# A first expert picked by ranking, and a sort that runs among its weight pieces

## The chip, the core and the metric

The program runs on one core of a Trainium2 chip: TensorE (PE), VectorE (DVE), ScalarE (ACT), GpSimd (POOL), and SyncE (SP), which here only issues DMAs. The metric is the device time of one execution in microseconds (us); less is better. The kernel before has a median of 1737.5 us over three runs, 1734.37 to 1741.73.

## What is computed

One layer over 1024 tokens of 1024 features in float32: an input projection; three mixers side by side (retention, a state-space scan, windowed attention); an output projection with a residual and a norm; then sixteen experts, each of which chooses its own 128 tokens:

```
mix  = concat(retention, S5, windowed attention) @ W_out
h    = LN(alpha*h + mix)
aff  = softmax(h @ router_w)                  # 1024 tokens x 16 experts
gates, idx = top_k(aff of one expert, 128)    # for each expert
xs   = h[idx]
out  = (silu(xs @ w_gate) * (xs @ w_up)) @ w_down * gates
h    = LN(alpha*h + scatter_add(out, idx))
```

Which tokens an expert takes is known only when all 1024 affinities of that expert are. A tie goes to the lower token number.

## The kernel before

The tokens lie in eight tiles of 128. After the mixers a loop over half steps i runs attention_scores (i), attention_out (i - 1), out_proj_half (i - 4) and router (i - 9): the stages of one tile follow one another with these lags, and a scheduler at build time merges them into a fixed order on each engine. A matmul in float32 at full rate takes three passes over numbers split in a high and a low part (mm3, L78): ACT rounds the high part, DVE subtracts to get the low one (split, L67; lines L71 and L72). This is done to activations and to every weight.

attention_out (L780) divides the four heads' probabilities S by their sum on DVE (L790), turns them on PE and multiplies them with the values. out_proj_norm stores the normed rows to h1_dram and, times alpha, to acc_dram. router (L852) turns the normed tile and multiplies it with the router's weights.

When the loop has ended, top_k (L910) finds for all experts at once the 128th largest affinity: on DVE eight rounds of MAX8 and MATCH_REPLACE, bitonic merges (L886, L887), then transposes and products on PE that give each token its slot. expert_hot and expert_slots turn slots into token numbers, expert_gather (L1005) fetches the 128 rows of one expert by an indirect DMA on POOL's queue, turned (L1019) transposes them on PE and tokens splits them into xT.

The experts' order is written by hand (Experts, L1043). Weights come as 384 pieces of 1 MB; of each quarter of an expert four pieces are for gate and up (tile gu), and two for the down projection (tile y) of the quarter before. load(k) issues the DMA of piece k on SP's queue into a raw buffer, and cut(k) splits it into a whl buffer, of which there are six. quarter (L1145) runs a piece's twelve matmuls on PE, then cuts the piece six further on. start (L1093) loads eight pieces and cuts six before the first; the low parts of the first three are done by POOL (POOL_FIRST = 3), the others by DVE. plan puts the other steps (silu, hid, its turn to hT, the next expert's tokens) between the pieces.

Of the kernel before, what the change touches and what calls it, by code (L numbers as in the profile page):

```python
# [779 lines left out]
def attention_out(K, i):  # L780
# [71 lines left out]
def router(K, t):  # L852
    nc, pool = K.nc, K.op
    z = K.Y.pop(t)[2]
    hT = K.rt.pop(t)[:, 1, :].rearrange("p (c f) -> p c f", c=KC)
    for q in range(2):
        pt = K.ptp.tile([P, 4, P], F32, name="tp")
        for c in range(4):
            nc.tensor.transpose(pt[:, c, :], z[:, (q * 4 + c) * P:(q * 4 + c + 1) * P], K.ident)
        if q == 0 or t < NT - 1:  # L860
            nc.scalar.activation(hT[:, q * 4:q * 4 + 4, :], pt, AF.Copy)
        else:
            nc.vector.tensor_copy(hT[:, q * 4:q * 4 + 4, :], pt)
    pr = K.psm.tile([P, P], F32, name="sm")
    for c in range(KC):
        nc.tensor.matmul(pr[0:E, :], K.rw[:, c, :], hT[:, c, :], start=(c == 0), stop=(c == KC - 1))  # L866
    lT = pool.tile([E, P], F32, name="lT", bufs=2)
    nc.vector.tensor_copy(lT, pr[0:E, :])
    pl = K.psm.tile([P, E], F32, name="sm")
    nc.tensor.transpose(pl, lT, K.ident[0:E, 0:E])  # L870
    s = pool.tile([P, 4], F32, name="rsm", bufs=2)
    a = pool.tile([P, E], F32, name="aff", bufs=2)
    nc.vector.tensor_reduce(s[:, 0:1], pl, AX.X, OP.max)
    nc.vector.tensor_scalar(s[:, 1:2], s[:, 0:1], -1.0, None, op0=OP.mult)
    nc.scalar.activation(a, pl, AF.Exp, bias=s[:, 1:2], accum_out=s[:, 2:3])
    nc.vector.reciprocal(s[:, 3:4], s[:, 2:3])
    nc.vector.tensor_scalar(K.aff[:, t, :], a, s[:, 3:4], None, op0=OP.mult)


def bitonic(K, pool, x, rows, k, name):  # L880

    nc = K.nc
# [27 lines left out]
def top_k(K):  # L910
# [5 lines left out]
    aff = K.aff.rearrange("p t e -> p (t e)")
    with K.tc.tile_pool(name="topk", bufs=1, side="left") as pool:
        pt = K.ptp.tile([P, 4, P], F32, name="tp")
        nc.tensor.transpose(pt[:, 0, :], aff, K.ident)
        rest = [K.aff] + [pool.tile([P, NT, E], F32, name=f"rest{i}") for i in range(2)]  # L920
        for i in range(3):
            nc.gpsimd.tensor_copy(K.tok[:, :, :, 2 + i], rest[i])
            if i < 2:
                nc.gpsimd.tensor_tensor(rest[i + 1], rest[i], K.tok[:, :, :, 2 + i], OP.subtract)
        w = [[pool.tile([P, 64], F32, name=f"w{h}{i}") for i in range(2)] for h in range(2)]
        half = [pool.tile([P, 64], F32, name=f"half{h}") for h in range(2)]
        for h in range(2):
            nc.vector.tensor_copy(w[h][0], pt[:, 0, h * 64:(h + 1) * 64])
        for i in range(8):
            for h in range(2):  # L930
                nc.vector.max(half[h][:, i * 8:i * 8 + 8], w[h][i % 2])
            for h in range(2):
                if i < 7:
                    nc.vector.match_replace(w[h][1 - i % 2], half[h][:, i * 8:i * 8 + 8], w[h][i % 2], -1.0)
        both = pool.tile([P, P], F32, name="both")
        nc.vector.tensor_tensor(both[:, 0:64], half[0], half[1][:, ::-1], OP.max)
        nc.vector.tensor_tensor(both[:, 64:P], half[0], half[1][:, ::-1], OP.min)
        top = bitonic(K, pool, both, P, 32, "b128")
        for rows in (64, 32):
            o = pool.tile([rows, P], F32, name=f"o{rows}")  # L940
            nc.vector.tensor_copy(o, top[rows:2 * rows, ::-1])
            m = pool.tile([rows, P], F32, name=f"m{rows}")
            nc.vector.tensor_tensor(m, top[0:rows], o, OP.max)
            top = bitonic(K, pool, m, rows, 64, f"b{rows}")
        rev = pool.tile([32, P], F32, name="rev")
        nc.vector.tensor_copy(rev, top[:, ::-1])
        pt = K.ptp.tile([P, 4, P], F32, name="tp")
        nc.tensor.transpose(pt[:, 0, 0:32], top, K.ident[0:32, 0:32])
        nc.tensor.transpose(pt[:, 1, 0:32], rev, K.ident[0:32, 0:32])
        m = pool.tile([P, 2, E], F32, name="mm")  # L950
        nc.vector.tensor_copy(m[:, 0, :], pt[:, 0, 0:E])
        nc.vector.tensor_tensor(m[:, 1, :], m[:, 0, :], pt[:, 1, E:2 * E], OP.max)
        pt = K.ptp.tile([P, 4, P], F32, name="tp")
        nc.tensor.transpose(pt[0:E, 0, :], m[:, 1, :], K.ident)
        tau = pool.tile([E, 1], F32, name="tau")
        nc.vector.tensor_reduce(tau, pt[0:E, 0, :], AX.X, OP.min)
        taus = pool.tile([E, P], F32, name="taus")
        nc.vector.tensor_copy(taus, tau.to_broadcast([E, P]))
        pt = K.ptp.tile([P, 4, P], F32, name="tp")
        nc.tensor.transpose(pt[:, 0, 0:E], taus, K.ident[0:E, 0:E])  # L960
        g = pool.tile([P, 2, NT, E], BF16, name="g")
        for i, op in ((0, OP.is_gt), (1, OP.is_equal)):
            nc.vector.tensor_tensor(g[:, i], K.aff, pt[:, 0, None, 0:E].to_broadcast([P, NT, E]), op)

        pp = K.pmm.tile([P, 512], F32, name="mm")
        before = pp[:, 0:2 * NT * E].rearrange("p (a t e) -> p a t e", a=2, e=E)
        n = pp[:, 2 * NT * E:2 * NT * E + E]
        nc.tensor.matmul(pp[:, 0:2 * NT * E], K.order01[:, 0, :], g.rearrange("p a t e -> p (a t e)"),
                         start=True, stop=False)
        for s in range(1, NT):  # L970
            nc.tensor.matmul(before[:, :, s:, :], K.order01[:, 1, :], g[:, :, 0:NT - s, :],
                             start=False, stop=(s == NT - 1))
        pn = K.psm.tile([P, E], F32, name="sm")
        for t in range(NT):
            nc.tensor.matmul(pn, K.order01[:, 1, :], g[:, 0, t, :], start=(t == 0), stop=(t == NT - 1))
        w = pool.tile([P, 4, NT, E], F32, name="sl")
        nc.vector.tensor_copy(w[:, 0], before[:, 0])
        nc.vector.tensor_copy(w[:, 3, 0], pn)
        nc.vector.tensor_tensor(w[:, 1], before[:, 1], w[:, 3, 0:1].to_broadcast([P, NT, E]), OP.add)
        nc.vector.tensor_tensor(w[:, 0], w[:, 0], w[:, 1], OP.subtract)  # L980
        nc.vector.tensor_tensor(w[:, 0], w[:, 0], g[:, 0], OP.mult)
        nc.vector.tensor_tensor(w[:, 1], w[:, 1], w[:, 0], OP.add)
# [544 lines left out]
```

## Time and profile before

| | |
|---|---|
| median of three runs | 1737.5 us |
| the profiled execution | 1739.56 us |
| its span, first to last instruction | 1737.9 us |
| attention and projection loop | about 360 to 527 us |
| last routers, sort, first gather | 527 to 585 us |
| experts | 585 to 1720 us |

Times in the rows are microseconds from the start of the span. PE's busy time counts pipelined matmuls whose ends are modelled, so it can be full while single matmuls are further apart than they need to be. A chain row gives what the end of the program can be followed back to.

### The profile page before, as it was taken

Reading aid. Unit: us, or ns where it says so; the run is one execution under the profiler, and the core shown is the slowest. Engines: PE = TensorE matmul, PEld = TensorE weight load, DVE = VectorE, ACT = ScalarE, POOL = GpSimd, SP = SyncE. Lnnn points to the kernel's source line nnn. Section 1 sums busy time; section 2 is a strip of 40 time slices with the busy share of each in tenths; the row PEclk is TensorE's granted clock in tenths of the full one; section 3 lists DMA queues with packets and bytes.
Section 4 is the critical chain, followed back from the end, with each engine's and each line's share of the span. In section 5 each row is a group of like instructions: output and inputs, shape, how many; then the busy total and the mean of one; then the engine's idle time right before and its main releaser. Section 6 shows DMA issues by size and latency. Waiting matters only on the chain.

```text
span 1737.9 us, 21027 instructions
## 1 busy us (share of the span) xinstructions
PE 1608.6 (93%) x7673; PEld 1294.0 (74%) x7673; DVE 1435.3 (83%) x1678; ACT 1058.7 (61%) x1082; POOL 335.5 (19%) x403
## 2 busy tenths in 40 slices
PE   6898996899993599999999999999999999999996
PEld 4688875577772488888888888888888778778785
DVE  8687962678867688888888889888898999989995
ACT  3332331455543377777777777777777777777772
POOL 6926801001003101011010010110101213121121
PEclk9999898999997699999999999999999999999998
DMA  6353189652225399999999999999999999999993
GB/s 246 115 143 102 51 244 267 196 176 74 77 105 242 113 337 370 371 387 356 382 377 370 383 362 376 382 371 383 366 372 409 384 396 412 382 406 376 394 402 138
DMA packets 110871, 512.53 MB, mean 295 GB/s; under 512 B 12336, under 2 KB 35120, under 8 KB 60080
## 3 DMA queue, kind: packets, MB, share of 16 engines
q1 hardware_dynamic: 100640, 481.31, 73.1%
q0 software_dynamic: 10128, 29.89, 5.6%
q8 instruction: 60, 0.98, 0.2%
q14 instruction: 43, 0.35, 0.1%
HBM read 465.01 MB, written 46.14 MB: 294 GB/s over the span
## 4 chain that ended last, share of the span: by engine, by line
PE 58%; DVE 14%; DMA 12%; issue 7%; ACT 4%; POOL 3%; SPq 1%; POOLq 0%; DVEq 0%; ACTq 0%
PE gu L1038 28%; PE y L1038 13%; DVE whl L72 5%; DMA zz<-acc_d 4%; PE mm L80 3%; PE mm L82 3%; PE mm L81 3%; ACT whl L71 2%; DMA wraw<-in_exp_w_down 2%; DMA wraw<-in_exp_w_up 2%; PE tp L1023 2%; PE tp L796 1%; PE sm L866 1%; PE po L81 1%; PE po L82 1%
## 5 line engine op out<-in xcount | busy, mean ns | idle before, releaser
L72 DVE TENSOR_TENSOR whl<-wraw,whl 128x2048 fp32r<-128x2048 f32 (+1 forms) x395 | 887.0, 2256 | 136.2 <-ACT whl L71 135.8
L71 ACT ACTIVATE whl<-wraw 128x2048 fp32r<-128x2048 f32 (+1 forms) x400 | 753.3, 1887 | 260.3 <-PE gu L1038 124.1
L1038 PE MATMUL gu<-whl,xT 128*128 128x512 f32 x3072 | 748.5, 400 | 0.0
L1038 PEld LDWEIGHTS gu<-whl,xT 128*128 128x128 f32 x3072 | 573.1, 189 | 130.7 <-ACT xT L71 0.3
L1038 PE MATMUL y<-whl,hT 128*128 128x512 f32 x1536 | 369.0, 396 | 0.7 <-ACT hT L71 0.7
L1038 PEld LDWEIGHTS y<-whl,hT 128*128 128x128 f32 x1536 | 288.6, 188 | 70.6 <-ACT hT L71 0.9
L1014 POOL DMA_INDIRECT xs<-h_d,index x16 | 44.8, 2798 | 755.9 <-issue 492.7
L80 PE MATMUL mm<-hT,whl 128*128 128x512 f32 x160 | 63.6, 398 | 6.2 <-DVE qst L75 5.3
L82 PE MATMUL mm<-hT,whl 128*128 128x512 f32 x160 | 63.1, 394 | 0.0
L81 PE MATMUL mm<-hT,whl 128*128 128x512 f32 x160 | 63.0, 393 | 0.0
L71 ACT ACTIVATE hT<-tp 128x512 fp32r<-128x512 f32 x80 | 46.4, 585 | 24.5 <-PE tp L141 15.4
L72 DVE TENSOR_TENSOR hT<-tp,hT 128x512 fp32r<-128x512 f32 x80 | 54.2, 681 | 7.1 <-ACT hT L71 7.1
L80 PE MATMUL mm<-WO,yh 128*128 128x512 f32 x128 | 51.2, 400 | 2.7 <-ACT yh L71 2.7
L80 PE MATMUL mm<-whl,hT 128*128 128x512 f32 (+1 forms) x128 | 47.3, 371 | 4.2 <-ACT gate L326 1.8
L81 PE MATMUL mm<-WO,yh 128*128 128x512 f32 x128 | 50.4, 393 | 0.0
L82 PE MATMUL mm<-WO,yl 128*128 128x512 f32 x128 | 50.1, 398 | 0.0
L1023 PE MATMUL tp<-ident,hid 128*128 128x128 f32 x256 | 38.8, 274 | 9.2 <-DVE hid L1122 9.1
L1023 PEld LDWEIGHTS tp<-ident,hid 128*128 128x128 f32 x256 | 31.2, 140 | 20.4 <-DVE hid L1122 12.6
L82 PE MATMUL mm<-whl,hT 128*128 128x512 f32 (+1 forms) x128 | 46.3, 363 | 0.0
L81 PE MATMUL mm<-whl,hT 128*128 128x512 f32 (+1 forms) x128 | 46.3, 364 | 0.0
L776 ACT ACTIVATE S<-S,asm 128x384 f32<-128x384 f32 (+1 forms) x64 | 36.9, 579 | 12.5 <-DVE asm L772 12.4
L1122 DVE TENSOR_TENSOR hid<-hid,gu 128x512 f32<-128x512 f32 x64 | 43.5, 679 | 0.0
(386 smaller groups left out, 1832.1 us busy)
## 6 DMA issues: line engine op xcount, KB each, us to landing
wraw<-in_exp_w_gate SPq DMA_DIRECT2D x128, 1024.0 KB, 7.4
wraw<-in_exp_w_up SPq DMA_DIRECT2D x128, 1024.0 KB, 7.2
wraw<-in_exp_w_down SPq DMA_DIRECT2D x128, 1024.0 KB, 8.0
wraw<-in_w_in SPq DMA_DIRECT2D x8, 1024.0 KB, 6.3
x<-in_x SPq DMA_DIRECT2D x8, 512.0 KB, 5.0
h_d<-x SPq DMA_DIRECT2D x8, 512.0 KB, 2.9
wraw<-in_w_out SPq DMA_DIRECT2D x4, 1024.0 KB, 5.7
q_d<-qst SPq DMA_DIRECT2D x64, 64.0 KB, 3.6
```

What stands on the lines that cost most here:

```text
L71: nc.scalar.activation(hi, src, AF.Copy)
L72: eng.tensor_tensor(lo, src, hi.bitcast(F32), OP.subtract)
L80: nc.tensor.matmul(ps, a[0], b[0], start=start, stop=False)
L81: nc.tensor.matmul(ps, a[0], b[1], start=False, stop=False)
L82: nc.tensor.matmul(ps, a[1], b[0], start=False, stop=stop)
L776: nc.scalar.activation(S[g][:, :W], S[g][:, :W], AF.Exp, bias=nm[:, g:g + 1], accum_out=rs[:, g:g + 1])
L796: nc.tensor.transpose(pt[:, g, :], S[g][:, (b - b0) * P:(b - b0 + 1) * P], K.ident)
L866: nc.tensor.matmul(pr[0:E, :], K.rw[:, c, :], hT[:, c, :], start=(c == 0), stop=(c == KC - 1))
L1014: nc.gpsimd.indirect_dma_start(out=xs, out_offset=None, in_=K.h1_dram, in_offset=bass.IndirectOffsetOnAxis(ap=K.index[:, e:e + 1], axis=0))
L1023: K.nc.tensor.transpose(pt[:, c, :], src[:, (c0 + c) * P:(c0 + c + 1) * P], K.ident)
L1038: nc.tensor.matmul(ps, a[s][c], u[:, t, i * w:(i + 1) * w], start=first and id(ps) not in began, stop=last and left[id(ps)] == 0)
L1122: at(self.after, q, 3, lambda: nc.vector.tensor_tensor(self.h[q], self.h[q], self.pg[q][1], OP.mult))
```

## The change

Five parts, and a rearrangement of the loop that goes with them:

1. The router no longer waits for the norm: its weights are multiplied by the norm's gain once, and mean and deviation are applied to the 16 logits (affinities). The lags become 1, 3 and 5. The division of S goes from DVE to ACT.
2. For the first expert alone, each tile's tokens are ranked by counting how many tokens have a larger affinity (rank_tile). When seven tiles are counted, their best 128, the candidates, are fetched by an indirect DMA while PE still projects the last tile (candidates_ranked, candidates_fetched).
3. When the last tile's affinities are there, first_slots counts them against the candidates, and first_turned picks the 128 rows of the first expert out of the two tiles by products with one-hot matrices, which turns them at once.
4. cut is divided into high (ACT) and low (DVE), which run ahead by lead(n) pieces; the first pieces are cut in the last tile's section (last_tile), which is written in a fixed order.
5. top_k, now a generator, gives one slice of the sort of all experts after each piece of the first expert. The second expert's gather moves to the third quarter.

```
     for g in range(4):
-        nc.vector.tensor_scalar(S[g][:, :W], S[g][:, :W], rd[:, g:g + 1], None, op0=OP.mult)
+        nc.scalar.activation(S[g][:, :W], S[g][:, :W], AF.Copy, scale=rd[:, g:g + 1])
...
+def rank_before(K, row, t, col, own):
+    G = K.tk.tile([P, LT * P], BF16, name="G")[:, 0:row.shape[1]]
+    nc.vector.tensor_scalar(G, row, K.aff[:, t, 0:1], None, op0=OP.is_ge, op1=OP.add, accum_out=K.cnt[:, t, col:col + 1])
...
+def candidates_fetched(K):
+    for t in range(LT):
+        nc.tensor.matmul(pt[:, 0, 0:5], K.hot0[:, t, :], K.tok[:, t, 0, :], start=(t == 0), stop=(t == LT - 1))
...
+    nc.gpsimd.indirect_dma_start(out=K.xc, out_offset=None, in_=K.h1_dram[0:LT * P, :],
+                                 in_offset=bass.IndirectOffsetOnAxis(ap=index, axis=0))
...
+def first_turned(K, half):
+    src = (K.Y[LT][2], K.xc)
+    for c in range(4):
+        cs = slice((half * 4 + c) * P, (half * 4 + c + 1) * P)
+        for i in range(2):
+            K.nc.tensor.matmul(pt[:, c, :], src[i][:, cs], K.hits[i], start=(i == 0), stop=(i == 1))
...
+    def low(self, k):
+        while self.lows <= min(k, len(self.order) - 1):
+            k1, self.lows = self.lows, self.lows + 1
+            u, raw = self.whl[k1], self.raw.pop(k1).rearrange("p a b -> p (a b)")
+            self.K.nc.vector.tensor_tensor(u[:, 1, :], raw, u[:, 0, :].bitcast(F32), OP.subtract)
+            if k1 != 2:
+                self.load(k1 + (2 if k1 < 2 else 5))
...
+    def lead(self, n):
+        return 3 + sum(n >= i for i in (16, 30, 44))
...
-            self.cut(self.taken + self.RING)
+            if self.sort and next(self.sort, self) is self:
+                self.sort = None
+                K.sorted()
+            lead = self.taken + self.lead(self.taken)
+            self.high(min(lead + 1, self.taken + self.RING))
+            self.low(lead)
...
+def last_tile(K, I, O, pool, close):
...
+    affinities(K, t)
+    token_parts(K, t)
+    out_proj_part(K, LT, 0, 7, KC)
+    G = rank_tile(K, t)
+    out_proj_part(K, LT, 1, 0, 4)
+    router_turn(K, LT, 0)
+    candidates_ranked(K, G)
+    out_proj_part(K, LT, 1, 4, 6)
+    candidates_fetched(K)
+    router_part(K, LT, 0)
+    X.high(1)
+    out_proj_part(K, LT, 1, 6, KC)
+    out_proj_stats(K, LT)
...
+    first_slots(K)
+    out_proj_store(K, LT)
+    halves = [first_turned(K, half) for half in range(2)]
+    pt = first_numbers(K)
+    rows = top_k_rows(K)
+    X.low(1)
...
+    for half in range(2):
+        X.tokens(0, half, halves[half])
+        if half == 0:
+            for k in range(4, 8):
+                X.load(k)
+            X.high(3)
+    X.low(2)
+    expert_gather(K, 0, pt)
+    X.sort = top_k(K, rows)
```

In DVE's order before, from the end of the sort to the first expert's matmuls (sl and slot are the sort's last tiles, hot the one-hot tiles, slotc and index the token numbers):

```order
L984 SCALAR_TENSOR_TENSOR slot<-sl 128x128
L992 TENSOR_TENSOR hot<-slot,slots 128x512 x2
L1009 COPY slotc<-tp 128x5
L1010 TENSOR_TENSOR index<-slotc 128x1
L1011 TENSOR_TENSOR slotc<-slotc 128x1
L1012 TENSOR_TENSOR gates<-slotc 128x1
L72 TENSOR_TENSOR whl<-wraw,whl 128x2048 x3
L72 TENSOR_TENSOR xT_5480<-tp,xT_5479 128x512 x2
```

In DVE's order of the changed kernel, from the last hit tile into the sort (w and half are the sort's first tiles):

```order
L1100 TENSOR_SCALAR hit_5438<-slots,last 128x128
L1303 TENSOR_TENSOR whl<-wraw,whl 128x2048
L71 TENSOR_TENSOR xT_5495<-tp,xT_5494 128x512 x2
L1303 TENSOR_TENSOR whl<-wraw,whl 128x2048
...
L1148 MATCH_REPLACE w_5532<-half_5536,w_5533 128x64
L1148 MATCH_REPLACE w_5534<-half_5537,w_5535 128x64
L1303 TENSOR_TENSOR whl<-wraw,whl 128x2048
L1145 MAX half_5536<-w_5532 128x8
L1145 MAX half_5537<-w_5534 128x8
```

The tokens of the first expert stood behind the whole sort and three subtractions; now they stand ahead of the sort, which begins after the third piece and is cut by the subtractions of the pieces that follow.

In ACT's order before, around the first expert's tokens xT:

```order
L71 ACTIVATE whl<-wraw 128x2048 x6
L71 ACTIVATE xT_5479<-tp 128x512 x2
L71 ACTIVATE whl<-wraw 128x2048 x2
L1116 ACT_TABLE_LOAD
L1116 ACTIVATE hid<-gu 128x512
```

And in ACT's order of the changed kernel (ah is the last tile times alpha, hitb the one-hot tiles in bfloat16):

```order
L932 ACTIVATE ah<-z 128x1024
L1119 ACTIVATE hitb_5465<-hit_5437 128x128
L1119 ACTIVATE hitb_5466<-hit_5438 128x128
L70 ACTIVATE xT_5494<-tp 128x512
L1296 ACTIVATE whl<-wraw 128x2048
L70 ACTIVATE xT_5494<-tp 128x512
L1296 ACTIVATE whl<-wraw 128x2048 x2
```

Six pieces were cut ahead of the tokens, which came in one go; now the upper part of piece 3 stands between the two halves of the tokens.

In PE's order of the changed kernel, from ahead of the third gate-and-up piece of the third quarter (g, taus and mm are tiles of the sort, the sort's products of g are left out):

```order
L1181 MATMUL tp<-ident,taus 128x16
L1256 MATMUL gu<-whl,xT_5494 128x512 x4
L1256 MATMUL gu<-whl,xT_5495 128x512 x4
L1256 MATMUL gu<-whl,xT_5494 128x512 x4
L1189 LDWEIGHTS order_147
L1189 MATMUL tp<-g,order_147 128x256
...
L1256 MATMUL gu<-whl,xT_5494 128x512 x4
L1256 MATMUL gu<-whl,xT_5495 128x512 x4
L1256 MATMUL gu<-whl,xT_5494 128x512 x4
L1217 LDWEIGHTS hot
L1217 MATMUL tp<-tok,hot 128x5
```

Before, all products of the sort stood ahead of the first gu matmul. Now PE comes to them between pieces, and each waits there for the slice of the sort on DVE that makes its operand; the products of the one-hot tiles (hot) stand ahead of piece 14.

## Rows read from the trace of the kernel before

**Rows 1.** Windows by stage: length, busy (instructions) per engine, PEclk, DMA share, GB/s.
```profile
360.00:527.00 167.00, 165.49 (x875) 130.06 (x876) 126.78 (x334) 79.57 (x199) 14.69 (x15) 1.00 0.28 92
527.00:541.00 14.00, 8.69 (x69) 6.63 (x67) 7.65 (x22) 3.69 (x11) 1.70 (x2) 0.99 0.26 89
541.00:572.00 31.00, 2.82 (x21) 1.74 (x20) 27.07 (x108) 11.05 (x6) 15.54 (x8) 0.50 0.71 298
572.00:585.00 13.00, 2.70 (x17) 2.28 (x18) 8.65 (x10) 0.78 (x2) 2.93 (x1) 0.50 0.53 202
585.00:602.00 17.00, 14.21 (x63) 11.00 (x63) 10.69 (x13) 10.16 (x8) 0.52 (x1) 0.89 0.05 9
602.00:1720.00 1118.00, 1109.63 (x5025) 893.28 (x5024) 999.73 (x652) 829.99 (x603) 137.77 (x80) 1.00 0.98 376
```

**Rows 2.** Chain that ended last, loop and seam: start, us, what.
```profile
340.94 0.53 DVE S L790 x2
...
526.98 0.24 PE mm L82
...
546.53 1.12 DVE both L936
...
547.91 4.51 DVE b L886
552.42 4.47 DVE b L887
...
574.63 8.13 DMA xs<-h_d,index
...
584.78 10.32 PE gu L1038 x36
```

**Rows 3.** Groups of instructions by form, 602 to 1720: busy us, mean ns, idle before.
```profile
L72 DVE TENSOR_TENSOR whl<-wraw,whl 128x2048 fp32r<-128x2048 f32 x375 | 854.2, 2289 | 114.1 <-ACT whl L71 114.0
...
L71 ACT ACTIVATE whl<-wraw 128x2048 fp32r<-128x2048 f32 x374 | 717.8, 1922 | 251.9 <-PE gu L1038 118.8 <-PE y L1038 67.7 <-DMA wraw<-in_exp_w_down 24.0
...
L72 DVE TENSOR_TENSOR hT<-tp,hT 128x512 fp32r<-128x512 f32 x64 | 43.7, 683 | 2.6 <-ACT hT L71 2.6
```

**Rows 4.** Timeline of PE around pieces 14 and 15.
```profile
632.35 5.77 PE L1038 MATMUL y<-whl,hT 128*128 128x512 f32 x24
637.96 0.60 PE L1023 MATMUL tp<-ident,hid 128*128 128x128 f32 x4
```

**Rows 5.** Timeline after the last projection matmul: norm, router.
```profile
529.01 1.27 DVE L62 SCALAR_TENSOR_TENSOR z<-z,l1mv,g 128x1024 f32<-128x1024 f32 x1
529.23 1.45 POOL L61 TENSOR_TENSOR l1rs<-l1rs,mhalf 128x1 f32<-128x1 f32 x1 [14.58 <-DVE l1rs L60]
...
533.40 1.92 PE L866 MATMUL sm<-rt,rw 128*16 128x128 f32 x16 [0.19 <-ACT aff L875]
```

**Rows 6.** Groups by form in the loop, 360 to 527.
```profile
L776 ACT ACTIVATE S<-S,asm 128x384 f32<-128x384 f32 x40 | 24.2, 606 | 9.1 <-DVE asm L772 9.1
...
L790 DVE TENSOR_SCALAR S<-S,asm 128x384 f32<-128x384 f32 x44 | 15.7, 413 | 0.2
```

**Rows 7.** DMA issues, 560 to 640: KB each, median us to landing.
```profile
wraw<-in_exp_w_gate SPq DMA_DIRECT2D x5, 1024.0 KB, 4.8
```

**Rows 8.** Timeline of DVE: begin and end of the sort.
```profile
541.32 0.36 DVE L928 COPY w<-tp 128x64 f32<-128x64 f32 x2 [0.63 <-PE tp L919]
...
565.42 0.21 DVE L946 COPY rev<-b 32x128 f32<-32x128 f32 x1
```

**Rows 9.** Head of the page.
```profile
span 1737.9 us, 21027 instructions
```

**Rows 10.** Windows around the rise of PE's clock.
```profile
541.00:587.00 46.00, 7.52 (x43) 5.54 (x43) 37.61 (x120) 12.24 (x8) 18.46 (x9) 0.50 0.63 258
587.00:590.00 3.00, 3.00 (x11) 2.42 (x10) 0.34 (x1) 0.42 (x1) 0.00 (x0) 0.74 0.02 5
...
595.00:600.00 5.00, 3.20 (x21) 2.30 (x20) 3.58 (x2) 4.77 (x4) 0.00 (x0) 1.00 0.00 0
```

More of the change, by code (lines that the diff above doesn't have):

```diff
@@ L728, in attention_keys @@
     nc = K.nc
-    K.KHL = [K.hl.tile([P, 2, L], F32R, name=f"KHL{kv}", tag="whl") for kv in range(2)]
-    K.AV = K.hl.tile([P, 2, NT, P], F32R, name="AV", tag="whl")
+    K.KHL = [K.kv.tile([P, 2, L], F32R, name=f"KHL{kv}") for kv in range(2)]
+    K.AV = K.kv.tile([P, 2, NT, P], F32R, name="AV")
     for kv in range(2):
@@ L852, in router, with bitonic @@
 def router(K, t):
-    nc, pool = K.nc, K.op
-    z = K.Y.pop(t)[2]
-    hT = K.rt.pop(t)[:, 1, :].rearrange("p (c f) -> p c f", c=KC)
     for q in range(2):
[L857 to L882, printed above, removed]
+        router_turn(K, t, q)
+    for q in range(2):
+        router_part(K, t, q)
+    affinities(K, t)
+    out_proj_gain(K, t)
+    out_proj_shift(K, t)
+    out_proj_store(K, t)
+def bitonic(K, pool, x, rows, k, per):
+    nc, n = K.nc, 0
     while k:
-        y = pool.tile([rows, P], F32, name=name, bufs=2)
+        if n and n % per == 0:
+            yield
+        n += 1
+        y = pool.tile([P, P], F32, name="b", bufs=2)[0:rows]
         a, b = (v.rearrange("p (n two k) -> p n two k", two=2, k=k) for v in (x, y))
@@ L907, in top_k_consts, with token_parts @@
     K.slot = cp.tile([P, NT, E], F32, name="slot")
-def top_k(K):
+def token_parts(K, t):
     nc = K.nc
[L916 to L926, printed above, removed]
-        for h in range(2):
[L928 to L982, printed above, removed]
-        nc.vector.tensor_tensor(w[:, 2], g[:, 0], g[:, 1], OP.add)
-        nc.vector.scalar_tensor_tensor(K.slot, w[:, 2], -float(L), w[:, 1], op0=OP.mult, op1=OP.add)
@@ new lines, in first_slots @@
+def first_slots(K):
+    nc, tk, t = K.nc, K.tk, LT
+    row = rank_row(K, K.aff[:, t, 0:1])
+    G = rank_before(K, K.crow, t, 0, None)
+    ps = K.ptp.tile([P, 4, P], F32, name="tp")
+    nc.tensor.matmul(ps[:, 0, 0:1], G, K.order01[:, 1, 0:1], start=True, stop=True)
+    rank_before(K, row, t, 2, row)
+    r = tk.tile([P, 2], F32, name="last")
+    K.hits = [tk.tile([P, P], F32, name=f"hit{i}") for i in range(2)]
+    nc.vector.tensor_reduce(r[:, 0:1], K.cnt[:, t], AX.X, OP.add)
+    nc.vector.tensor_scalar(K.hits[0], K.slots, r[:, 0:1], None, op0=OP.is_equal)
+    nc.vector.scalar_tensor_tensor(r[:, 1:2], ps[:, 0, 0:1], -1.0, K.place, op0=OP.mult, op1=OP.add)
+    nc.vector.tensor_scalar(K.hits[1], K.slots, r[:, 1:2], None, op0=OP.is_equal)
@@ L1170, in quarter @@
                 fn()
-            self.cut(self.taken + self.RING)
+            if self.sort and next(self.sort, self) is self:
[4 more added lines that the diff above has]
+            self.low(lead)
             self.taken += 1
         self.pg.pop(q - 1, None), self.h.pop(q - 2, None), self.hT.pop(q - 2, None)
-def experts(K, I, O):
-    X = Experts(K, I, O)
-    T = mybir.EngineType
-    with K.tc.manual_schedule(engines={T.PE, T.Activation, T.DVE, T.Pool, T.SP}):
-        X.start()
-        for q in range(4 * E + 1):
-            X.quarter(q)
-        last_rows(X, E - 1)
-    assert not X.before and not X.after
+def last_tile(K, I, O, pool, close):
+    nc, X, t = K.nc, K.X, LT - 1
+    for q in range(2):
+        router_turn(K, t, q)
+    out_proj_gain(K, t)
+    out_proj_shift(K, t)
+    X.high(0)
+    X.low(0)
+    out_proj_part(K, LT, 0, 0, 4)
+    for q in range(2):
+        router_part(K, t, q)
+    out_proj_store(K, t)
+    out_proj_part(K, LT, 0, 4, 7)
+    affinities(K, t)
+    token_parts(K, t)
[10 more added lines that the diff above has]
+    out_proj_stats(K, LT)
+    router_turn(K, LT, 1)
+    out_proj_gain(K, LT)
+    router_part(K, LT, 1)
+    X.high(2)
+    affinities(K, LT)
+    token_parts(K, LT)
+    close(*K.psums)
+    c_py, K.py = pool("py", space=PSUM, bufs=2)
+    c_pg, K.pg = pool("pg", space=PSUM, bufs=3)
+    c_pt, K.ptp = pool("ptp2", space=PSUM, bufs=3)
+    first_slots(K)
[4 more added lines that the diff above has]
+    X.low(1)
+    return halves, pt, rows, (c_pt, c_pg, c_py)
 def expert_add(K, e, py):
@@ new lines, in build @@
+        t, n = divmod(i - 5, 2)
+        if 0 <= t and n == 0:
+            router(K, t)
+        t, n = divmod(i - 3, 2)
+        if 0 <= t:
+            out_proj_part(K, t, n)
+            if n == 1:
+                out_proj_stats(K, t)
+    close(c_at2, c_kv)
+    c_hla, hla = pool("hla", side="right", bufs=3)
+    T = mybir.EngineType
+    hold = tc.manual_schedule(engines={T.PE, T.Activation, T.DVE, T.Pool, T.SP})
+    hold.__enter__()
+    hl = [hla] * 3
+    K.next_hl = lambda k: hl[k % 6]
@@ L1470, in layout, with sorted_out @@
+    X.low(2)
+    expert_gather(K, 0, pt)
+    X.sort = top_k(K, rows)
+    raw0 = []
+    def sorted_out():
+        close(c_sel)
+        raw0.append(pool("raw0", bufs=3))
+        K.raw0 = raw0[0][1]
+    K.sorted = sorted_out
+    for q in range(4 * E + 1):
+        X.quarter(q)
+    last_rows(X, E - 1)
+    assert not X.before and not X.after and not X.sort
+    hold.__exit__(None, None, None)
+    close(raw0[0][0], c_raw2, c_ex, c_hlb, c_raw, c_con, c_hla, *psums)
 def layout(inputs):
```

357 lines of the change are left out of this document (267 added, 90 removed).

## The prediction

> **What bounds the kernel now.** I read four views in this order: busy time by stage, the chain of waits across the seam between the stages, the groups of instructions in the two dense stages, and the timeline of the seam. By stage [rows 1], two stretches are full of matmul: the attention and projection loop (PE busy 165.49 of 167 us) and the experts (1109.63 of 1118). Between them lie 75 us, from 527 to 602, in which PE is busy 28.4 us. The chain [rows 2] shows why: after the last projection matmul at 526.98 it runs through the last routers, the sort on DVE, and the gather of the first expert's rows (8.13 us), and the first expert matmul starts at 584.78. In the experts DVE is the second engine, 999.73 of 1118 us [rows 1], so it has about a tenth free; each weight piece costs it one 2.289 us subtraction and ACT 1.922 [rows 3], against 2.8 us on PE (24 matmuls, two pieces, from 632.35 to 637.96 [rows 4]). Since PE is the bound after the seam, the gain is the time by which the experts' pieces come earlier. I compare both kernels where PE ends piece 15 (pieces count from 0 in the order of use; piece 15 is the second down-projection piece in the third quarter's list): before, that is 638.0 [rows 4]. From there the same work follows in both.
>
> **The loop.** Added per tile: one transpose on PE, three or so counting passes on DVE, small token copies on POOL; each of the eight router products moves 16 columns instead of 128, and the transpose back goes; 64 scalings of the probabilities go from DVE to ACT. Because PE is full, I count PE's rows. From the common start of the loop to the first row of the last tile's section, the changed program has 48 projection matmuls fewer than before had at 527.2 (that half tile and the other one move behind the point): 48 x 0.233 = 11.2 us. It has 48 router matmuls where before had 40. Before's cost 0.243 each (16 instructions in 1.92 for eight [rows 5]); a new one lies between the 0.11 of its weight load, an estimate from half of that, and 0.243; I take 0.15, nearer the bottom since only 16 columns pass. That is -2.5 us, with +2.4 for 16 set-up products, +0.7 for six rank transposes, -1.2 for the back-transposes. The section then starts at 527.2 - 11.8 = 515.4 (call it zero), 510 to 521 by the bounds. The scalings leave DVE (413 ns each [rows 6]) and cost ACT an unseen scaled copy: more than nothing, at most the 606 ns of the exponential on the same tile [rows 6], so 0 to 39 us in sum; I take 0.5 each, 32 us. ACT is busy 79.57 of 167 us [rows 1], so it has room, and PE's own work covers it; I enter 0 and keep 0 to +15 (64 x (0.5 - 0.27), if ACT's extra over DVE's 0.27 back to back [rows 2] all came to lie on the path).
>
> **The last tile.** DVE sets this part. A pass over 512 columns costs it 0.68 [rows 3], over 1024 1.27 [rows 5]; counting passes with a sum are not in the trace, and lie between half of that rate (the scalings' 384 columns in 0.27) and the full one, which I take, being that of the other passes that also read PSUM or two tensors. From zero: tile 6's two norm passes, the five counting passes over earlier tiles, one weight subtraction (2.29) and the affinities of tile 6 end at about 10.6, while PE, with 24 projection matmuls and the router, is ready at 8.0; PE waits 2.7. The count over seven tiles, its rank and the one-hot tile (896 columns) end at 16.3; the index is there at 17.3 and POOL, whose five small copies of tile 6 stand in front and are done by then, lands the gather of the candidates 8.13 later [rows 2], at 25.4. Beside it PE finishes the projection at 19.9; then tile 7's statistics, the turn of its second half, the gain pass 1.27 with POOL's 1.45 beside it [rows 5], and the affinities end at 26.0, and the counts of the last tile give both hit tiles at 27.6. The gather, 2.2 us earlier, is hidden; were it as slow as 4 us more, it would cost 2.
>
> **Piece 0 to piece 15.** The rows are picked by 16 plain products of 128 columns (0.243 each by [rows 5], 3.9 us, twice that at the low clock). DVE next cuts piece 1 (to 29.9), and only then is piece 3 loaded: 4.8 us to landing [rows 7], so 34.9. Here lies a wait that the change adds. ACT's order has the upper half of piece 3 between the two halves of the tokens: what is queued behind the wait is the second half of xT, and DVE's lower half and PE's piece 1 wait for that. The token buffers also lie where the last tile's rows were, so xT waits for its two stores, which SP issues ahead of piece 3's load; issued by 26.8 and half as big as a load, they are down by about 30, and hide behind piece 3. Pieces 4 to 7 load after the picking. So ACT cuts piece 3 until 36.9, xT's second half is there at 37.5, and DVE's half at 38.2. DVE then has, in its order, up to the tile that PE needs ahead of piece 14: 14 subtractions, 14 x 2.29 = 32.1; the whole sort; two hid and two hT passes, 4 x 0.68 = 2.7; four one-column instructions, 0.6 (none over the 0.21 of the copy in [rows 8]); the one-hot tiles of expert 1, 1.3 (two passes of 512 columns, 0.68 each). The sort: from 541.32 to 565.63 is 24.3 us [rows 8], but three of its instructions ran beside POOL's subtractions and took 1.12, 4.51 and 4.47 [rows 2] where their like take about 0.63 together; POOL's subtractions go, so 24.3 - 10.1 + 0.6 = 14.8, and 2.3 more for the passes after the transposes, now five fewer. 17.1 in all. Sum 38.2 + 32.1 + 17.1 + 2.7 + 0.6 + 1.3 = 92.0; then PE has the counts 0.4 and pieces 14 and 15, 5.6: 98.0. On the chip's scale that is 515.4 + 98.0 = 613.4 against 638.0, 24.6 us earlier. PE alone, at its 2.8 a piece from 37.5, would have been there at 82, so this stretch is DVE's, and PE waits some 16 us in it.
>
> Two things are free here. Weight loads: 1 MB goes by in about 2.8 us at the experts' 376 GB/s [rows 1], and DVE's pace is near 4 us a piece. The gather for expert 1 is issued at about 96 and needed before piece 19, at 107, 11 us against 8.13.
>
> **Sum.** The profiled execution took 1739.6 us (span 1737.9 [rows 9]), 2.1 over the median of 1737.5. 1739.6 - 24.6 = 1715.0, or 1712.9 beside the median: 1713.
>
> **Rivals.** (a) The sort hides after all and PE keeps its own pace: 98 becomes 82, 16 us more gain, 1697. For it: piece 0 and 1 are cut ahead. Against: DVE's tenth of free time is 5 us in that stretch, and the sort is 17. (b) The attention loop grows. ACT's scaling stands between the exponentials and PE's transposes in one engine's order, so its 15 us come on the path: 1728. For: each scaling waits for a DVE reciprocal and blocks what ACT has behind it. Against: ACT has half of the stretch free. The Trainium skill, "ScalarE: Activation LUTs", Rules for kernel authors, says to multiply on VectorE and not on ScalarE; the rows above agree on the price per instruction, and by that rule this rival's 1728 would be the time. (c) Weights. start() loaded thirteen pieces ahead of the first; now three are there, and lead() has DVE cut three pieces ahead of PE instead of six until piece 16. If those three never come back, PE waits for weights later by 3 x 2.8 = 8 us, 1721. For: loads never pause in the experts. Against: DVE's tenth of free time refills them in some thirty pieces, and 376 GB/s there is what PE's pace asks for, not a limit that the rows show. (d) Slower: TensorE's clock. It stood at 0.50, which is 1.2 GHz, from 541 to 587, after PE had nearly nothing to do, and was back at 2.4 GHz only after 3 us of dense matmuls [rows 10]. If the waits of 1 us and more between pieces keep it at 1.2 GHz for the whole first expert, its 24 pieces take 5.6 us each, from 546 to 685, where before ended them at 661 (eight more pieces of 2.8): 24 us late, 1761. It decides from piece 16 on: until there, at 5.6 us each, both kernels are level. For it: the new stretch has PE waiting in every piece. Against: in 595 to 600 PE was busy 3.20 of 5 us and the clock stayed at 1.00 [rows 10]. The Trainium skill, "TensorE: Matmul & The Clock Gate", HAM oscillation, tells of kernels in which each burst after a wait began cold; by that rule the time would be this rival's, and the row from 595 speaks against it here.
>
> **How the numbers follow.** Forecast 0.48, its own range 1702 to 1724 (the start of the section by its bounds, 5 us either way, and 5 for the counting passes). (a) 0.13, (b) 0.16, (c) 0.13, (d) 0.05; 0.05 for a loop that loses the whole gain. The range 1697 to 1733 leaves out (d), the last and the edges of (a) and (b). A change under 0.5 per cent, 8.7 us, can't be told from none. Faster: the forecast, (a), (c) and half of (b), 0.82; same: the rest of (b) and half of the last, 0.10; slower 0.08.
>
> **What would show it.** Right: the last projection matmul near 535 (515.4 + 19.9), the first expert matmul near 546, a gap before the second piece ended by ACT's xT, DVE without idle time until the one-hot tiles, PE waiting for DVE's whl in pieces 3 to 13, piece 15 ending near 613, and the same rate after that. Wrong: a loop that ends later than 540 (then (b)); PE waiting for ACT's upper halves behind loads after 620 (c); a granted clock of 0.5 beyond 600 (d); PE dense from the second piece on (a).

## The result, and the profile after

The changed kernel took 1715.6 us (median of four runs, 1713.0 to 1722.0) against 1739.6 for the kernel before beside it (1734.4 to 1742.6): a ratio of 0.9871 with a 95% interval of 0.9831 to 0.9911, 1.3 per cent faster. A later set of runs gave the same ratio (0.9844 to 0.9897; 1719.3 against 1739.6). Forecast were 1713 and a range of 1697 to 1733. The profiled execution took 1713.6, its span 1711.9, against 1739.6 and 1737.9 [rows 9].

By stage, the changed kernel (windows; columns as in [rows 1]):
```profile
358.00:517.00 159.00, 155.06 (x834) 123.61 (x832) 110.39 (x303) 100.57 (x249) 15.60 (x41) 0.99 0.23 77
517.00:538.70 21.70, 17.88 (x100) 14.30 (x100) 14.32 (x37) 9.41 (x14) 3.32 (x11) 0.93 0.44 144
538.70:546.80 8.10, 2.34 (x15) 1.68 (x15) 7.22 (x21) 1.79 (x5) 1.70 (x6) 0.71 0.17 70
546.80:553.50 6.70, 6.65 (x34) 6.54 (x34) 2.50 (x3) 0.60 (x2) 0.00 (x0) 0.56 0.59 229
...
615.70:1690.00 1074.30, 1062.89 (x4863) 859.86 (x4862) 973.81 (x638) 806.90 (x588) 139.01 (x80) 1.00 0.98 383
```
From the last projection product to the first expert product it was 58 us before (526.98 to 584.78 [rows 2]); it is 17 now, with 6.65 us of picking in them. Behind piece 15 the picture is that of before.

PE's timeline at the marks (the changed kernel; start, us, line; in brackets the idle time before, and its releaser):
```profile
517.39 1.19 PE L885 MATMUL tp<-ident,z 128*128 128x128 f32 x8
...
546.80 6.62 PE L1110 MATMUL tp<-hit,z 128*128 128x128 f32 x32 [1.24 <-DVE hit L1098]
...
555.38 12.93 PE L1256 MATMUL gu<-whl,xT 128*128 128x512 f32 x48
572.42 0.66 PE L1241 MATMUL tp<-ident,hid 128*128 128x128 f32 x4 [4.11 <-DVE hid L1339]
...
610.01 5.84 PE L1256 MATMUL y<-whl,hT 128*128 128x512 f32 x24
```
The first row is the start of the last tile's section, the prediction's zero (forecast 515.4); the last one is pieces 14 and 15, which end near 615.7 (forecast 613.4; before 638.0 [rows 4]). That is 22.3 us earlier; the other 3.7 of the two spans' 26.0 come behind it (1096.2 us to the end against 1099.9). Each is one execution: in the thirteen profiles below, that last stretch takes 1095.4 to 1103.5 us, and in all but the first the section starts 4 us or more later. So the 3.7 shows nothing, and the 22.3 is good to some 5 us.

The chain that ended last, across the seam (start, us, what):
```profile
525.90 8.13 DMA acc_d<-ah
534.13 0.60 ACT rt L887
...
546.46 0.28 DVE hit L1098
547.05 2.30 DVE whl L1303
549.37 4.86 DMA wraw<-in_exp_w_up
554.25 1.91 ACT whl L1296
556.16 0.49 ACT xT L70
556.67 0.69 DVE xT L71
```
Two transfers stand in it. The lower five rows are the wait that the prediction described: DVE's piece 1 (547.05), then the load of piece 3, ACT's upper half of it, and behind that the second half of the tokens (xT). The first row it did not have: ACT's copy of the last tile's turned rows (rt) waits for a store of 8.13 us, because tile 6's scaled rows (ah) lie in the same buffer.

DVE's waits from there to the one-hot tiles (timeline, as above):
```profile
554.21 0.69 DVE L71 TENSOR_TENSOR xT<-tp,xT 128x512 fp32r<-128x512 f32 x1 [4.87 <-ACT xT L70]
556.67 0.69 DVE L71 TENSOR_TENSOR xT<-tp,xT 128x512 fp32r<-128x512 f32 x1 [1.77 <-ACT xT L70]
...
601.65 0.49 DVE L1184 TENSOR_TENSOR g<-aff,tp 128x128 bf16<-128x128 f32 x2 [0.18 <-PE tp L1181]
605.61 0.49 DVE L1199 SCALAR_TENSOR_TENSOR sl<-tp,g 128x128 f32<-128x128 f32 x2 [1.28 <-PE tp L1195]
```
After the second xT pass DVE stands still for 1.5 us in 52; before it, it is idle for 6.6.

### The profile page after: what moved, and what is told of

Read it like the earlier page. It is cut to its first block, busy times and chain, and to the rows that moved or that the text cites. A ratio compares the mean times of both kernels' runs of the same rounds, so it can differ in the third digit from the quotient of the medians.

```text
span 1711.9 us, 21285 instructions
## 1 busy us (share of the span) xinstructions
PE 1613.7 (94%) x7738; PEld 1308.9 (76%) x7738; DVE 1420.3 (83%) x1672; ACT 1089.9 (64%) x1157; POOL 321.5 (19%) x442
## 4 chain that ended last, share of the span: by engine, by line
PE 54%; DVE 16%; DMA 12%; issue 8%; ACT 5%; POOL 3%; SPq 1%; POOLq 0%; DVEq 0%; ACTq 0%
PE gu L1256 25%; PE y L1256 13%; DVE whl L1303 6%; DMA wraw<-in_exp_w_down 5%; DMA zz<-acc_d 3%; PE mm L79 3%; PE mm L81 3%; PE mm L80 3%; ACT whl L1296 2%; PE tp L1241 2%; PE tp L795 1%; DMA wraw<-in_exp_w_up 1%; DMA qs<-q_d 1%; PE at L765 1%; PE po L79 1%
## 5 line engine op out<-in xcount | busy, mean ns | idle before, releaser
L1303 DVE TENSOR_TENSOR whl<-wraw,whl 128x2048 fp32r<-128x2048 f32 x384 | 873.4, 2289 | 95.6 <-ACT whl L1296 95.2
L1296 ACT ACTIVATE whl<-wraw 128x2048 fp32r<-128x2048 f32 x384 | 734.7, 1917 | 241.3 <-PE gu L1256 75.1
```

Of the source, the lines that this page charges most:

```text
L1296: self.K.nc.scalar.activation(u[:, 0, :], self.raw[k1].rearrange("p a b -> p (a b)"), AF.Copy)
L1303: self.K.nc.vector.tensor_tensor(u[:, 1, :], raw, u[:, 0, :].bitcast(F32), OP.subtract)
```

## The experiments

All times are counted within a run from the start of the last tile's section (the x8 row above), since the section starts at 521.6 to 524.1 in the eleven other executions that have the same loop, and at 517.4 in the first. The loop is counted from the first projection product to that start. Columns: ratio to the kernel before, the loop, the first picking product, the end of the second xT pass, and the end of piece 15 (the next row of PE). "changed" is the kernel itself, in its first profile and once more.

| kernel | ratio (95%) | loop | picking | xT | piece 15 |
|---|---|---|---|---|---|
| changed | 0.9871 (0.9831 to 0.9911) | 167.7 | 29.4 | 40.0 | 98.3 |
| after_again | 0.9871 (0.9844 to 0.9897) | 167.7 | 30.7 | 41.3 | 98.0 |
| own_ah | 0.9862 (0.9840 to 0.9885) | 166.0 | 27.0 | 37.4 | 95.7 |
| tok_first | 0.9883 (0.9863 to 0.9903) | 167.6 | 29.8 | 38.2 | 97.3 |
| warm | 0.9859 (0.9814 to 0.9903) | 168.0 | 30.3 | 40.8 | 97.6 |
| warm_tok | 0.9883 (0.9851 to 0.9916) | 167.8 | 30.4 | 36.5 | 94.9 |
| hid_late | 0.9875 (0.9836 to 0.9913) | 168.0 | 30.7 | 41.2 | 98.0 |
| early | 0.9865 (0.9834 to 0.9895) | 167.8 | 29.8 | 40.3 | 93.4 |
| no_merge | 0.9857 (0.9836 to 0.9879) | 167.7 | 29.3 | 39.8 | 93.0 |
| sort_ahead | 0.9947 (0.9925 to 0.9970) | 165.0 | 29.6 | 40.2 | 110.6 |
| lead6 | 0.9905 (0.9877 to 0.9934) | 165.6 | 29.7 | 40.3 | 106.5 |
| dve_scale | 0.9855 (0.9817 to 0.9893) | 171.2 | 28.2 | 38.7 | 95.5 |
| best | 0.9832 (0.9806 to 0.9857) | 168.0 | 27.6 | 37.0 | 90.1 |

Where an edit reaches only later stages, the picking still varies from 29.3 to 30.7 and piece 15 from 98.0 to 98.3, so a difference under 0.7 us at piece 15 shows nothing. Behind piece 15 the profiles differ by 8 us, so a few us won there need not show in a time: warm_tok is 3 us earlier at piece 15, and its ratio is no better. Of the ratios, only that of sort_ahead is parted from the changed kernel's by its interval; the rest is read from the traces.

**The store under the turned rows (own_ah).**
```
-    ah = K.op.tile([P, D], F32, name="ah", tag="rt")
+    ah = K.op.tile([P, D], F32, name="ah", tag="rt") if t < LT - 1 else \
+        K.op.tile([P, D], F32R, name="ah", tag="yh", bufs=2).bitcast(F32)
```


> The scaled rows of tile 6 (ah) get a buffer that the turned rows of the last tile (rt) don't share, so ACT's first rt copy of the last tile no longer waits for the store of ah (8.13 us, landed at 534.03 in the changed kernel). Theory: that store lies on the path. The candidates' row on PE then follows DVE's candidate sums (533.6) and not ACT's rt, 1.1 us earlier, and the last projection matmuls stay at 2.4 GHz, another 1.2: the projection ends near 536.5 and not 538.8, and piece 15 ends 2.3 us earlier, near 613.4; the time falls by about 2 us. Rival: the gather of the candidates or the load of piece 3 sets the rest, and piece 15 stays at 615.7.

```profile
538.30 0.29 PE L1016 MATMUL tp<-ident,cand 128*128 128x128 f32 x1 [0.86 <-DVE cand L1080]
541.65 0.66 PE L885 MATMUL tp<-ident,z 128*128 128x128 f32 x4 [0.78 <-DVE z L841]
...
617.64 0.60 PE L1241 MATMUL tp<-ident,hid 128*128 128x128 f32 x4
```
In this PE timeline the candidates' row now waits for DVE's candidate sums and not for ACT's rt; tile 7's rows are turned 19.7 us after the section's start (22.2 in the changed kernel), and piece 15 ends at 95.7, 2.3 to 2.6 earlier. The store was on the path, with the price that was forecast for it: the candidates' row comes 1.0 earlier (16.4 after the start, 17.4 in the changed kernel), and the rest is won in the last projection products, where the granted clock stays at 1.00 (0.60 over 534.8 to 538.8 in the changed kernel).

**The wait for piece 3, and the clock (tok_first, warm, warm_tok).**
```
 tok_first:        for k in range(4, 8):
                       X.load(k)
-                  X.high(3)
+          X.high(3)                # behind both token halves
 warm:    +    warm(K, 10)          # unread products on PE
               first_slots(K)
          +    warm(K, 5)
```


> ACT copies both halves of the tokens (xT) before it cuts the upper half of piece 3. Theory, as predicted: the wait for piece 3's load stands in front of the second half of xT, and DVE's work behind it is the bound, so DVE restarts 1.8 us earlier (second xT pass ends near 555.5, not 557.3) and piece 15 ends near 613.9. Rival 1: PE's pace is the bound there, and piece 15 stays at 615.7. Rival 2: piece 3, now 0.6 us later, is missed by DVE, and piece 15 comes 0.6 later.

> Fifteen extra projection products with a result that nobody reads fill PE's two gaps before the picking (10 in the 2.5 us before tile 7's rank row, 5 in the 1.2 us before the first picking product), so that the granted clock should stay at 2.4 GHz. Theory: the picking shortens from 6.6 to some 4 us, but ACT's upper half of piece 3 stands between the token halves and its load, issued behind DVE's piece 1, lands at the same time as the picking ended; so the second xT pass and piece 15 stay where they are (within 0.5 us, counted from the start of the last tile's section). Rival: the picking at 1.2 GHz is what sets the tokens, and all behind it comes 2.5 us earlier.

> Both of two edits run before alone: the fifteen unread products that keep PE's clock up before the picking (alone: picking 4.0 and not 6.6 us, second xT pass no earlier), and both token halves ahead of ACT's upper half of piece 3 (alone: piece 15 1.0 us earlier). Theory: the picking and piece 3's load end at the same time, so each hides the other, and only both edits together bring the tokens forward: the second xT pass ends near 36.2 us from the section's start (39.9 in the changed kernel), and piece 15 comes 3 to 4 us earlier, at 94.3 to 95.3. Rival: the edits add up, 1.0 and 0.7 us, to 96.6.

ACT in warm (timeline): the tokens' first half, then piece 3.
```profile
556.37 0.60 ACT L70 ACTIVATE xT<-tp 128x512 fp32r<-128x512 f32 x1 [3.49 <-PE tp L1122]
559.63 1.91 ACT L1296 ACTIVATE whl<-wraw 128x2048 fp32r<-128x2048 f32 x1 [2.66 <-DMA wraw<-in_exp_w_up]
```
The picking shortens to 4.00 us, and ACT then stands 2.66 us for piece 3's load, so xT ends no earlier (40.8). tok_first alone brings xT forward by 1.8 against the first profile, and about half of it is lost again:
```profile
603.11 0.28 DVE L1176 TENSOR_REDUCE tau<-tp 16x1 f32<-16x128 f32 x1 [0.82 <-PE tp L1174]
```
DVE, early by then, waits 0.82 for a transpose that stands behind PE's pieces: 97.3, 0.7 to 1.0 earlier where 1.8 was forecast. With both edits xT ends at 36.5, and piece 15 at 94.9, 3.1 to 3.4 earlier; the rival's sum was 96.6. So the picking at 1.2 GHz and piece 3's load end together in the changed kernel (0.1 us apart in the first profile, 0.7 in the second), and each hides the other.

**Who sets the pace (no_merge, hid_late, early, lead6).**
```
 no_merge: -    while k:                     hid_late: + s = 2 if q == 0 else s
           +    while k > 99:
 early:    rows = top_k_rows(K)     # ahead of the picking, in a gu bank
           X.low(1)
      +    rows = top_k_rounds(K, rows)
 lead6:    - sum(n >= i for i in (16, 30, 44))    + (4, 8, 12)
```


> The bitonic merges of the sort are left out (26 steps, 52 DVE passes of at most 64 elements, 7.4 us in the trace of the changed kernel), so the thresholds of experts 1 to 15 are other numbers; all transfers and products stay in kind and size. Theory: DVE's work is the bound from the tokens to the one-hot tiles, so piece 15 ends 6 to 7.4 us earlier, near 609. Rival: PE or the loads of the weights set the pace, and piece 15 moves by less than 2 us.

> PE turns the first quarter's hid two pieces later (before piece 6, not before piece 4), so that its wait of 4.1 us for DVE's hid, with pieces 4 and 5 ready in the meantime, goes. Theory: DVE's work sets the pace up to the one-hot tiles, so PE's wait only moves: piece 15 ends within 0.7 us of the changed kernel's (98.3 us from the start of the last tile's section). Rival: the wait and the 3 us of 1.2 GHz behind it are lost PE time, and piece 15 ends 3 to 5 us earlier.

> PE turns the affinities for the sort ahead of the picking, and DVE runs the sort's eight rounds of maxima (5.1 us in the changed kernel, in slices behind pieces 2 to 4) right behind its piece 1, in the time in which it waited for ACT's xT (4.9 us). Theory: DVE's work is the bound up to the one-hot tiles and its idle time in front of the tokens is wasted, so filling it brings piece 15 forward by 4 to 5 us (to 93 to 94.5 us from the start of the last tile's section, 98.3 before), with the second xT pass not later than before. Rival: PE's own pace (pieces of 2.75 us, the wait for hid, the slow clock) is the bound, and piece 15 moves by less than 1.5 us.

> DVE's lead over PE grows from three pieces to six at pieces 4, 8 and 12 and not at 16, 30 and 44. Theory: each piece more of lead inside the stretch that DVE paces is one more subtraction of 2.2 us on the path, so piece 15 ends 4 to 6.6 us later, and since PE waits almost nowhere after it, the time is 3 to 6 us longer. Rival (the stock): the three pieces save PE's waits later on, and the time stays or falls by up to 4 us (all of PE's idle time behind piece 15 beyond that of the kernel before).

hid_late: PE's wait of 4.1 us goes and nothing comes earlier; PE stands 2.1 us for hT and three times 0.7 to 0.8 for DVE's subtractions instead. early: 4.6 to 4.9 us at piece 15 out of 5.1 us of work moved into DVE's idle time. lead6: three subtractions more, 8.2 to 8.4 us later, over the forecast's 6.6; the rows of PE show why:
```profile
618.94 0.27 PE L1217 MATMUL tp<-tok,hot 128*128 128x5 bf16 x4 [3.07 <-DVE hot L1208]
619.54 0.27 PE L1217 MATMUL tp<-tok,hot 128*128 128x5 bf16 x4 [0.33 <-DVE hot L1208]
619.67 8.54 PE L1256 MATMUL y<-whl,hT 128*128 128x512 f32 x24
```
After its wait of 3.07 us for the one-hot tiles, PE takes 8.54 us for pieces 14 and 15 that else take 5.84. Its ratio of 0.9905 stands for some 6 us, with an interval that overlaps the changed kernel's. no_merge, which leaves out the merges, fell short: 7.4 us of DVE's work removed gave 5.0 to 5.3. DVE waits 3.7 us for PE there on its way to the one-hot tiles, 2.2 more than in the changed kernel, and the last pieces run at PE's own pace:
```profile
597.55 11.32 PE L1256 MATMUL gu<-whl,xT 128*128 128x512 f32 x48
608.71 0.41 PE L1217 MATMUL tp<-tok,hot 128*128 128x5 bf16 x8
```
Four pieces in 11.3 us and no wait for the one-hot tiles. So DVE is the bound of the changed kernel, and PE, with the tokens where they are, comes next, some 5 us behind it.

**The slices undone (sort_ahead).**
```
-    X.sort = top_k(K, rows)
+    for _ in top_k(K, rows): pass
```


> The sort is not cut into slices among the pieces but runs whole between the token copies and piece 0. Theory: in the changed kernel the sort's 16 us of DVE time are not hidden, since DVE sets the pace of pieces 1 to 14; so undoing the slices costs less than the sort: PE starts piece 0 near 578 (559.5 and 0.6 for the first slots, 16 for the sort, some 2 for its three round trips to PE) and needs 16 pieces at 2.75 and 3 us of slow clock, so piece 15 ends at 622 to 626, 6 to 10 us later. Rival (the sort hides among the pieces): 18 us later, 634.

```profile
584.70 13.11 PE L1256 MATMUL gu<-whl,xT 128*128 128x512 f32 x48
...
633.20 0.60 PE L1241 MATMUL tp<-ident,hid 128*128 128x128 f32 x4
```
PE begins 62.1 us after the section's start (60.6 forecast) and needs 48.5 for 16 pieces: piece 15 ends 12.3 to 12.6 us later than in the changed kernel. That lies between the theory's 6 to 10 and the rival's 18. So about 12 of the 22.3 us at piece 15 are the slices. The other 10 or so belong to the rest of the change together: the loop, the router, the ranking, the early gather and POOL's subtractions; no run parts these.

**The scalings back on DVE (dve_scale).**
```
-        nc.scalar.activation(S[g][:, :W], S[g][:, :W], AF.Copy, scale=rd[:, g:g + 1])
+        nc.vector.tensor_scalar(S[g][:, :W], S[g][:, :W], rd[:, g:g + 1], None, op0=OP.mult)
```


> The 64 scalings of the probabilities go back from ACT to DVE. Theory: neither engine sets the pace of the attention loop, PE does (155 of 159 us busy), so the section of the last tile starts within 1.5 us of the same time, and the run's time is the same within 2 us. Rival (ACT's 0.59 against DVE's 0.40 lies on the path): the section starts 5 to 12 us earlier. Other rival: DVE, with the counting passes added, gets too full, and the section starts 3 us or more later.

The loop takes 171.2 us, 3 to 6 more than in the twelve other profiles, and not within 1.5 of them, so in this one profile the second rival holds there (DVE is busy 0.77 of the loop, 0.68 in the changed kernel). But the section behind it is 2.5 to 2.8 shorter (95.5), and the time is the same. Most of that the clock gave back: over the last projection products (543.17 to 545.69) it was 1.00, and the projection ends 19.8 us after the section's start, where it ends at 21.5 and 21.9 in the changed kernel's two profiles, with 0.60 over 534.8 to 538.8 in the first. Why the clock stood there is not settled.

**The three gains together (best, after_again).** Own buffer, tokens ahead of piece 3, and rounds ahead of the tokens.

> Three edits in one: the own buffer for tile 6's scaled rows (alone 2.6 us at piece 15), both token halves ahead of ACT's piece 3 (alone 1.0), the rounds of maxima in DVE's idle time (4 to 5 forecast). Theory: the first moves the section's end, the other two remove idle time of DVE in front of the same work, so they add up: piece 15 at 89 to 91 us from the section's start, 7 to 9 us earlier than in the changed kernel, and a time about 0.45 per cent below it. Rival: PE becomes the bound (16 pieces at 2.75 from first tokens at 36 to 38, and 3 to 4 us of slow clock and waits), and piece 15 stays above 92.

> The changed kernel once more, as a measure for the others of this call on the same chip. All theories: the times of its first runs within 0.3 per cent, the last tile's section 165 to 168 us behind the first projection product, piece 15 98 to 98.5 us behind the section's start.

DVE and PE in best:
```profile
557.43 1.29 DVE L71 TENSOR_TENSOR xT<-tp,xT 128x512 fp32r<-128x512 f32 x2 [0.44 <-issue]
```
```profile
573.42 1.12 PE L1239 MATMUL tp<-ident,hid 128*128 128x128 f32 x4 [4.77 <-DVE hid L1337]
...
611.87 0.60 PE L1239 MATMUL tp<-ident,hid 128*128 128x128 f32 x4
```
DVE's idle time ahead of the tokens is 0.44 us, and piece 15 ends at 90.1, 8 us earlier, in the forecast's 89 to 91. The time is 1711.6 us (1706.8 to 1714.4) against 1719.3 (1713.7 to 1722.2) of the changed kernel on the same chip, 7.7 less; the two ratios' intervals still overlap. It beats both kernels by median.

## Why the prediction was right

**The loop and its end: right within its bounds.** Forecast 515.4, measured 517.4. That it came so near is in part luck: in eleven later profiles with the same loop the section starts at 521.6 to 524.1, past the upper bound of 521. They part from the first ahead of the loop, whose first projection product stands at 349.7 in the first and at 353.7 to 357.6 in the others; how far the kernel before varies there, its one profile can't tell. Two terms were low, by 5.8 us in all, which would make the forecast 521.2. Groups of instructions in the loop of the changed kernel, and the set-up products on PE's timeline:
```profile
L897 PE MATMUL sm<-rwg,rt 128*128 128x16 f32 x96 | 11.6, 254 | 0.5 <-ACT rt L887 0.5
...
L789 ACT ACTIVATE S<-S,asm 128x384 f32<-128x384 f32 (+1 forms) x48 | 24.8, 587 | 2.2 <-DVE asm L787 1.8 <-DVE rsm L913 0.2
```
```profile
345.02 4.39 PE L873 MATMUL sm<-rwg,ones 128*128 128x16 f32 x32
```
A router product of 16 columns costs as much as one of 128: 1.85 us for eight, 0.23 each, not 0.15, which makes 3.8 us over 48; the 16 set-up products took 4.4 us, not 2.4. The scalings cost ACT 605 ns for 384 columns (587 is the mean with the shorter ones), all of the upper bound of 606 where 500 was taken, and were hidden.

**The last tile: one wait missed.** The counting passes run at the full rate that was chosen (1.13 us for 896 columns). The projection ended at 538.9, 21.5 after zero, where 19.9 was forecast, and the hits stood at 29.8 and not at 27.6. The step that fell short was the one on the stores: "they are down by about 30, and hide behind piece 3". That holds for tile 7's two stores, which nothing is seen to wait for. The prediction did not ask who waits for tile 6's, whose buffer ACT's rt takes 20 us earlier; own_ah puts 2.3 to 2.6 us on it.

**Piece 0 to piece 15: the mechanism right, one term hidden by chance.** Forecast were 92.0 - 38.2 = 53.8 us of DVE from the second xT pass to the one-hot tiles; it took 52.6 (557.28 to 609.84), 16.2 of them the sort's (17.1 forecast): 52.6 less 14 subtractions at 2.2 back to back, 2.4 for hid and hT, 1.7 for the small passes and the one-hot tiles, and 1.5 of waiting. So 98.3 us from zero to piece 15 for a forecast of 98.0 is in part two errors that cancel: the tokens came 1.8 late, and DVE took 1.2 less. PE spent 60.3 us on pieces that take 44.8 at 2.8, 15.5 more (some 16 forecast). The wait for piece 3 came where it was forecast: piece 3 landed 36.8 us after zero (34.9), and xT ended at 40.0 (38.2). Three of the prediction's own signs failed. PE never waited for DVE's subtractions between the pieces; it stood for hid (4.1 us), the merges (b, 1.8) and the one-hot tiles (1.2), and lost the rest to pieces at a low clock and to the products between them. There was no gap before the second piece. And the first expert product came at 555.4 and not at 546: the picking took 6.62 us (3.9 forecast at 2.4 GHz, 4.00 measured so in warm), at a granted clock of 0.56, and ACT's first xT waited for all of it (6.10 us for the last numbers' product), though its own half was done before. That fits token buffers that lie over what the picking reads, an overlap that the prediction saw for the stores alone; no run moves the buffers. It cost little, because the picking's end and piece 3's load came together (warm, warm_tok).

**The rivals.** (a), the sort hidden: no; filling or removing DVE's work moves piece 15 (early, no_merge). (b), ACT's scalings: the reverse; without them on ACT the loop is 3 to 6 us longer. The rule of the Trainium skill, "ScalarE: Activation LUTs", Rules for kernel authors, holds per instruction here (605 ns on ScalarE, 415 on VectorE in dve_scale, for 384 columns), but the loop was shorter with the slower engine; that a fuller DVE is the reason is argued from its busy share alone. (c), the stock: by the waits of PE behind piece 15, it stands 11.4 us for DVE's hid and one-hot tiles (9.6 of them six times for hid; 10.1 in after_again), where it stood 7.4 before, so 3 to 4 us and not 8 went there. A stock built earlier costs 8 us at piece 15, and no saving behind it shows (lead6). (d), the clock. Its sum was off: 24 pieces of 5.6 us from 546 end at 680, not 685, and its time would be some 1757. From the windows of the changed kernel:
```profile
556.00:558.00 2.00, 2.00 (x7) 1.52 (x6) 1.33 (x2) 0.64 (x2) 0.00 (x0) 0.52 0.99 410
...
560.00:566.00 6.00, 6.00 (x27) 4.82 (x26) 6.00 (x35) 5.31 (x5) 0.00 (x0) 1.00 0.96 396
...
574.00:576.00 2.00, 2.00 (x6) 1.63 (x5) 2.00 (x2) 2.00 (x2) 0.00 (x0) 0.50 0.95 393
...
578.00:580.00 2.00, 2.00 (x10) 1.65 (x9) 2.00 (x2) 0.00 (x0) 0.00 (x0) 1.00 0.88 352
...
594.40:596.00 1.60, 1.60 (x6) 1.31 (x5) 1.56 (x4) 1.23 (x2) 0.00 (x0) 0.50 1.00 420
...
608.00:612.00 4.00, 2.78 (x19) 1.92 (x18) 4.00 (x5) 2.36 (x2) 0.00 (x0) 1.00 0.63 213
```
And PE's wait for b, in the changed kernel and then in warm:
```profile
593.20 0.24 PE L1167 MATMUL tp<-ident,b 32*128 32x32 f32 x1 [1.82 <-DVE b L958]
...
594.39 4.21 PE L1256 MATMUL gu<-whl,xT 128*128 128x512 f32 x12
```
```profile
598.62 0.25 PE L1167 MATMUL tp<-ident,b 32*128 32x32 f32 x1 [1.87 <-DVE b L958]
...
599.46 3.00 PE L1256 MATMUL gu<-whl,xT 128*128 128x512 f32 x12
```
Behind the first pieces it fell to 0.50 twice: after the wait of 4.1 us for hid, back at 1.00 some 6 us later, and after the wait of 1.8 us for b. After the 0.9 us for the one-hot tiles it stayed at 1.00. What the Trainium skill, "TensorE: Matmul & The Clock Gate", HAM oscillation, tells of, a burst that begins cold after each wait, shows here behind some waits only: in warm the clock stayed at 1.00 after the same wait for b. The first fall cost nothing, DVE being the bound (hid_late). The second has a price. From the second xT pass to piece 15 it is 56.7 to 56.8 us in after_again, warm, hid_late and dve_scale, where the clock stayed at 1.00 there, and 58.3 to 59.1 in the changed kernel's first profile, own_ah, tok_first and warm_tok, where it fell and DVE then waited 1.5 to 2.3 us for PE. This is why after_again has its tokens 1.3 us later and piece 15 no later, and it is a part of what tok_first lost.

## What to carry to other kernels

Before a buffer's tag is shared, list who writes it next and whether a store still reads it: such a wait belongs to the next writer, however far from the store it stands. When two waits end together, an edit that removes one shows nothing, and only both edits in one run tell what they cost. Work spread among the pieces of a pipeline is free only as far as its engine has time left; fill that engine's idle time ahead of the stretch first.

## What the runs showed of the hardware

The price of an fp32 product of 16 columns did not fall below that of one of 128 (0.23 and 0.243 us): the columns that pass were not what it is made of. And a wait of PE can cost again behind it, in slow matmuls: 2.7 us after one of 3.1 (8.54 for 5.84 us in lead6), 1.6 after one of 4.1 (12.95 for 11.32 us of four pieces, in the changed kernel). It does not follow from the wait alone: after waits of 1.82 and 1.87 us for the same tile, the next piece took 4.21 us in the changed kernel (clock 0.50) and 3.00 in warm (1.00).
